# A transformer layer on one NeuronCore: the mixer's weight matrices laid out by the host in the blocks in which they are fetched

## The chip, the cores and the metric

The kernel runs on one core of one Trainium2 chip. The metric is the device time of one execution in microseconds (us), lower is better. All arrays come from HBM and the result goes back to HBM; what the host does to the inputs before the launch is not in the time.

## The reference

One layer on a sequence of 256 rows of 1024, in float32. A conditioning vector gives six modulation vectors. The mixer runs a gated linear recurrence and causal attention side by side on the modulated rows, and a mixture of 32 experts, two for each row, follows. Cut to what matters here:

```
mod = silu(c) @ w_ada + b_ada                  # w_ada 1024 x 6144: sh1, sc1, g1, sh2, sc2, g2
u    = normalize(x) * (1 + sc1) + sh1
proj = u @ w_in                                # w_in 1024 x 2560: x, y, q, k, v, 512 columns each
h    = rg_lru(conv(x)) * gelu(y)               # recurrence over time
att  = attention(q, k, v)
mix  = concat(rmsnorm(h), rmsnorm(att)) @ w_out   # w_out 1024 x 1024
x    = layernorm(alpha * x + g1 * mix)
x    = layernorm(alpha * x + g2 * experts(normalize(x) * (1 + sc2) + sh2))   # w1, w3, w2 of 32 experts
```

## The kernel before

**Slots.** An arena in SBUF holds five slots of 128 partitions x 4096 floats (16 KB of each partition, 2 MiB in all) and some work space; `slot(i)` is one of them. Each piece of a weight matrix that the mixer needs fills a slot and is used up before the next piece is fetched there. The experts' weights later use the same slots and three further buffers (`last`, `misc`, `fifth`).

**Fetches.** `load` (L224) fetches one slot in two DMAs of 1 MiB, one for each half of the partition's 16 KB. Which rows and columns go there is a rearranged view of the matrix in HBM (L220 to L222): the vectors sc1 (`V1[1, a]`, L254) come as 8 rows x 512 columns a partition, the vectors sh1, sc2 and g2 (`load_vec`) as 4 rows x 1024 columns, g1 and sh2 together (`load_ada`) as 2 rows x 2048 columns, the projections (`load_win`) as 8 rows x 512 columns, the output matrix (`load_wo`) as 4 rows x 1024 columns. So a partition's run of bytes that lie side by side in HBM is 2, 4, 8, 2 and 4 KB long in these five. The experts' w1, w3 and w2 lie in HBM so that a partition's 8 KB are one run.

**Order.** The program is written in the order in which each engine runs it; there is no planner. All of these fetches are issued by SyncE (SP) and go through one DMA queue, in order. SP waits before a fetch until the slot's last reader is done, and everything behind it waits too. The order at the start is x, `V1[1, 0]` (slot 0), half of W["x"] (slot 2), `V1[1, 1]` (slot 1), the other half of W["x"], `V1[0, 0]` and `V1[0, 1]` (slots 3 and 4), then W["y"] into slot 0 (L455), `pack_b`, W["q"] (L460), and so on: `AD[1, q]` (g1 and sh2), W["k"], W["v"], w_out, `V1[4]` and `V1[5]` (sc2 and g2).

**What uses them at the start.** TensorE transposes the normalized x, `scale_mm(0)` (L365) multiplies `V1[1, 0]`, `proj_T(0, ...)` (matmuls L430) projects x with W["x"]. Ahead of the matmuls each row block of a projection is split into two float32r parts, the high one by ScalarE (L407 or L410) and the rest by VectorE (L408 or L411). `vec_cols(0)` (L381, L387) turns `V1[0, 0]` and `V1[0, 1]` into the shift; VectorE adds it in L465, L467 copies it, L481 multiplies it with W["x"], and the projection of y begins. Between `vec_cols(0)` and L465 stands `ahead(9)` (L459): VectorE's L408 on the first row block of W["y"] comes ahead of L465 on its queue.

**Later.** Two modulation vectors go through HBM and back (`mod2_out` L660, `mod2_in` L664, both on SP; SP waits in L664 until the first has landed). The fetches of the first experts' weights (`load_static`, L859) need expert numbers that VectorE writes in L562 and SP reads (L856). The long run of expert units (L1212, L1355) fetches 8 KB rows in `bring_all` (L1166, L1169), the last group in halves.

Of the kernel before, what the change touches and what calls it, by code (L numbers as in the profile page):

```python
# [21 lines left out]
S, D = 256, 1024  # L22
H, DH = 8, 64
NE, DE = 32, 256
KD = D // 128
# [112 lines left out]
def arrays_of(inputs):  # L138
    i = {k: np.asarray(v) for k, v in inputs.items()}
    a, b, wg, rb, ln = pack_inputs(i)  # L140
    r = {k: np.ascontiguousarray(i[k]) for k in ("x", "w_ada", "w_in", "w_out", "w1", "w3", "w2")}
    r["b_ada"] = np.ascontiguousarray(i["b_ada"].reshape(12, 512))
    r["pack_a"], r["pack_b"], r["w_gate"], r["rb"], r["ln"] = a.array(), b.array(), wg, rb, ln
    return r, a.at, b.at
# [3 lines left out]
def layer(ctx: ExitStack, tc: tile.TileContext, at_a, at_b, x, w_ada, b_ada, w_in, w_out, w1, w3, w2,  # L148
          pack_a, pack_b, w_gate, rb, ln, out, dbg=None):
    nc = tc.nc  # L150
    te, ve, se, ge, sy = nc.tensor, nc.vector, nc.scalar, nc.gpsimd, nc.sync
# [34 lines left out]
    def slot(i):  # L186
        return arena[:, i * 4096:(i + 1) * 4096]
# [6 lines left out]
    def bank(pool=None):  # L194
        turn[0] += 1
        return (pool or (psx, psp)[turn[0] % 2]).tile([128, 512], F32, name="b")
# [11 lines left out]
    def A(name):  # L208
        o, w = at_a[name]
        return pka[:, o:o + w]  # L210
# [6 lines left out]
        o = at_a["par"][0] + PAR[name] + m  # L217
        return pka[:, o:o + n]

    ada = w_ada[0].rearrange("(p k) n -> p k n", k=KD)  # L220
    win = w_in[0].rearrange("(k p) n -> p k n", p=128)
    wov = w_out[0].rearrange("(k p) n -> p k n", p=128)  # L222

    def load(s, src):  # L224
        n, w = src.shape[1:]
        t = (slot(s) if isinstance(s, int) else s).rearrange("p (k n) -> p k n", k=n)
        for h in range(2):
            q = slice(h * n // 2, (h + 1) * n // 2)
            sy.dma_start(t[:, q], src[:, q])
        return t  # L230

    def load_vec(v, q, s):
        return load(s, ada[:, 4 * q:4 * q + 4, v * D:(v + 1) * D])

    def load_ada(g, q, s):
        return load(s, ada[:, 2 * q:2 * q + 2, g * 2048:(g + 1) * 2048])

    def load_win(j, s):
        return load(s, win[:, :, j * 512:(j + 1) * 512])

    def load_wo(j, s):
        return load(s, wov[:, 4 * j:4 * j + 4])

    se.dma_start(pka, pack_a)
    rbt = misc[:NB + 1, 3072:3464]
# [3 lines left out]
    AD, W = {}, {}  # L249
    V1 = {}  # L250

    W["x"] = slot(2).rearrange("p (k n) -> p k n", k=KD)
    for a in range(2):
        V1[1, a] = load(a, ada[:, :, D + a * 512:D + a * 512 + 512])  # L254
        sy.dma_start(W["x"][:, 4 * a:4 * a + 4], win[:, 4 * a:4 * a + 4, 0:512])
    V1[0, 0] = load_vec(0, 0, 3)
    V1[0, 1] = load_vec(0, 1, 4)
    ident = A("ident")

# [117 lines left out]
    def vec_cols(v):  # L377
        pa = abank()
        for k in range(KD):
            for j in range(4):  # L380
                te.matmul(pa[32 * j:32 * j + 32, 0:256], cd[:, k], V1[v, k // 4][:, k % 4, j * 256:(j + 1) * 256],  # L381
                          start=(k == 0), stop=(k == KD - 1), skip_group_check=True, tile_position=(0, 32 * j))
        r = tmp.tile([128, 256], F32, name="row", bufs=1)
        ve.tensor_copy(r, pa[:, 0:256])
        p = bank(psx)
        for s in range(2):
            te.matmul(p[:, s:8:2], r[:, s * 128:(s + 1) * 128], sel4, start=True, stop=True)  # L387
        return p[:, 0:8]
# [10 lines left out]
    def rows_of(w, scale=None):  # L399
        units.extend((w, k, scale) for k in range(KD))  # L400
# [18 lines left out]
    def proj_T(u, pool, after=None, mid=None, most=None, late=()):  # L419
        bs = [bank(pool) for _ in range(2)]  # L420
        for k in range(KD):
            ahead(most(k) if most else u + k + 4)
            t = split[u + k]
            products = [(m, a, b) for m in range(4) for a, b in parts3]
            if k in late:
                products.sort(key=lambda v: v[1])
            for n, (m, a, b) in enumerate(products):
                if mid and n == 6:
                    mid(k)
                te.matmul(half(bs, m), t[:, a, m * 128:(m + 1) * 128], ul[:, b, k], start=(k + m % 2 + a + b == 0),  # L430
                          stop=(k == KD - 1 and a == 1), skip_group_check=True)
            if after:
                after(k)
        return bs
# [18 lines left out]

    px = proj_T(0, psp, after_x, mid_x, lambda k: 4 if k < 4 else 8, (0, 4))
    W["y"] = load_win(1, 0)  # L455
    sy.dma_start(pkb, pack_b)
    rows_of(W["y"])
    p = vec_cols(0)
    ahead(9)  # L459
    W["q"] = load_win(2, 3)  # L460
    sy.dma_start(wgt, w_gate)
    ge.memset(brows[:, 0], 0.0)
    sy.dma_start(brows[0:128:32, 0], b_ada[4:8])
    AD[1, 0] = load_ada(1, 0, 1)
    ve.tensor_add(mod1[:, 0], p, A("bcol")[:, 0:8])  # L465
    shd = misc[:, 3072:3328].rearrange("p (k n) -> p k n", k=KD)
    ve.tensor_copy(shd, mod1[:, 0, :, None].to_broadcast([128, KD, 32]))  # L467
# [11 lines left out]
    for k in range(KD):  # L479
        j = k % 4  # L480
        te.matmul(pb[32 * j:32 * j + 32], shd[:, k], W["x"][:, k], start=(k < 4), stop=(k >= 4), skip_group_check=True,  # L481
                  tile_position=(0, 32 * j))
    W["k"] = load_win(3, 2)
    sy.dma_start(T, bass.AP(tensor=vrd.tensor, offset=vrd.offset, ap=[[1, 128], [384, H], [1, 256]]))
    AD[1, 1] = load_ada(1, 1, 4)
    rowx = brows[:, 1]
    xb = ch.tile([128, 4], F32, name="xb")
    xl, xc = t4(0), t4(1)
# [86 lines left out]
    def ada_mm(g, q, pt):  # L575
        for k in range(2):
            for j in range(4):
                te.matmul(pt[32 * j:32 * j + 32], cd[:, 2 * q + k], AD[g, q][:, k, j * 512:(j + 1) * 512],  # L578
                          start=(q == 0 and k == 0), stop=(q == 3 and k == 1), skip_group_check=True, tile_position=(0, 32 * j))
# [83 lines left out]
    def mod2_in(t, i):  # L663
# [3 lines left out]
    kT = nx[:, 1].rearrange("p (m t) -> p m t", m=4)  # L667
    pa1 = abank()
    ada_mm(1, 0, pa1)
    AD[1, 2] = load_ada(1, 2, 1)  # L670
    rows_of(W["k"])
    pq = proj_T(16, psp, after_q)
    AD[1, 3] = load_ada(1, 3, 3)
    qh = [qT[:, 2 * b:2 * b + 2].rearrange("p a b -> p (a b)") for b in range(2)]
    se.activation(qh[0], pq[0], AF.Copy, scale=DH ** -0.5)
    ve.tensor_scalar(qh[1], pq[1], DH ** -0.5, None, op0=OP.mult)
    ada_mm(1, 1, pa1)
    V1[4, 0] = load_vec(4, 0, 4)
    rows_of(W["v"])
    ge.memset(brows[:, 1], 0.0)  # L680
    sy.dma_start(brows[0:128:32, 1].rearrange("p (v n) -> p v n", v=2),
                 b_ada[8:12].rearrange("(v a) (h n) -> (a h) v n", v=2, h=2))
    pk = proj_T(24, psp, after_k)
    wo = [load_wo(0, 2)]
    ada_mm(1, 2, pa1)
    ada_mm(1, 3, pa1)
    wo.append(load_wo(1, 1))
    V1[4, 1] = load_vec(4, 1, 3)
    for b in range(2):
# [436 lines left out]
    p = bank(psp)  # L1126
# [66 lines left out]
    for k in range(KD):  # L1193
        q, sc, sh = pgs[k // 4][:, k % 4 * 128:k % 4 * 128 + 128], mod2p[:, 1, k:k + 1], mod2p[:, 0, k:k + 1]
# [551 lines left out]
```

## Time and profile before

| | |
|---|---|
| median of 3 runs | 307.99 us (307.07 to 308.94) |
| the profiled execution | 308.57 us, of which its span (first to last instruction) is 306.8 us |
| TensorE busy | 279.2 us (91%) |
| VectorE, ScalarE, GpSimd busy | 183.0, 108.9, 24.4 us |
| moved by DMA | 112.22 MB, mean 366 GB/s |
| granted TensorE clock | 0.99 on average |

How to read it: an engine's busy time tells how much of the span it worked, not whether the work sets the end. Two resources stand near full here, TensorE and the DMA engines, so the profile must be read stage by stage: which wait ends last there. L12 is line 12 of the kernel; `out<-in` names the tiles; SPq is SyncE's queue. A DMA's time to landing runs from its issue and contains all that stands ahead of it in the queue.

### The profile page before, as it was taken

The numbers are of one execution on the slowest core, as the hardware profiler recorded it, in microseconds if no ns is written. First come the engines' busy times: TensorE is split into PE (matmuls) and PEld (weight loads), VectorE is DVE, ScalarE is ACT, GpSimd is POOL, SyncE is SP. The second block draws the span as 40 slices with busy tenths as digits, with TensorE's granted clock in tenths as the row PEclk, the third lists the DMA queues.
The fourth block names the chain that finished last, engine by engine and source line by source line (L and its number), as shares of the span: only waits on it lengthen the run. The fifth ranks groups of instructions, "written<-read, shape, count | busy, mean of one in ns | idle before, by whom it ended". The sixth has DMA issues, their size and how long they took to land.

```text
span 306.8 us, 6105 instructions
## 1 busy us (share of the span) xinstructions
PE 279.2 (91%) x2344; PEld 186.3 (61%) x2344; DVE 183.0 (60%) x445; ACT 108.9 (35%) x230; POOL 24.4 (8%) x62
## 2 busy tenths in 40 slices
PE   0799999999999999999998999999999999959980
PEld 0578679897957644566475578585648455715430
DVE  2766188927786785888698790636273516250490
ACT  1233188778745452051438241123112211210110
POOL 0100632000010000000120200000000001200000
PEclk9999999999999999999999999999999999997998
DMA  7999999999999699899979999999999999999104
GB/s 271 388 392 407 395 396 401 385 394 426 406 409 407 237 419 418 316 424 347 311 246 424 366 414 425 420 420 424 420 419 421 418 420 420 422 412 395 49 4 146
DMA packets 26163, 112.22 MB, mean 366 GB/s; under 512 B 2253, under 2 KB 3586, under 8 KB 17420
## 3 DMA queue, kind: packets, MB, share of 16 engines
q1 hardware_dynamic: 25424, 110.74, 91.3%
q10 hardware_dynamic: 636, 0.99, 0.9%
q8 instruction: 20, 0.33, 0.4%
q14 instruction: 19, 0.16, 0.1%
q0 software_dynamic: 64, 0.01, 0.0%
HBM read 110.51 MB, written 1.22 MB: 364 GB/s over the span
## 4 chain that ended last, share of the span: by engine, by line
PE 57%; DMA 26%; DVE 11%; issue 1%; ACT 1%; POOL 0%; SPq 0%; DVEq 0%; ACTq 0%
DMA arena<-in_w 12%; PE b L430 11%; PE m L1212 10%; PE b L804 7%; DMA misc<-in_w 6%; DMA arena<-in_w_in 6%; PE m L1355 5%; PE b L779 4%; PE m L1286 3%; PE a L578 2%; PE a L1212 2%; PE acc L1309 2%; PE a L590 2%; DMA pka<-in_pack_a 1%; PE a L365 1%
## 5 line engine op out<-in xcount | busy, mean ns | idle before, releaser
L430 PEld LDWEIGHTS b<-ul,w 128*128 128x128 f32 x384 | 46.6, 192 | 4.2 <-ACT w L407 1.7
L430 PE MATMUL b<-ul,w 128*128 128x256 f32 x384 | 48.4, 285 | 0.5 <-ACT w L410 0.5
L1212 PE MATMUL m<-arena,xg 128*64 128x256 f32 (+1 forms) x288 | 38.4, 401 | 3.8 <-DMA arena<-in_w 3.8
L1212 PEld LDWEIGHTS m<-arena,xg 128*64 128x64 f32 (+1 forms) x288 | 21.9, 131 | 14.1 <-DMA arena<-in_w 4.7
L408 DVE TENSOR_TENSOR w<-arena,w 128x512 fp32r<-128x512 f32 x32 | 21.9, 698 | 13.9 <-ACT w L407 13.7
L1355 PE MATMUL m<-arena,hT 128*32 128x512 f32 (+2 forms) x184 | 29.1, 596 | 0.5 <-ACT hT L1333 0.5
L804 PE MATMUL b<-arena,mT 128*128 128x512 f32 x64 | 29.0, 601 | 0.0
L407 ACT ACTIVATE w<-arena 128x512 fp32r<-128x512 f32 x32 | 19.5, 625 | 12.4 <-DMA arena<-in_w_in 6.3
L1327 DVE TENSOR_TENSOR hh<-hh,m 128x256 f32<-128x256 f32 x7 | 2.9, 421 | 34.7 <-ACT hh L1326 34.7
L1212 PE MATMUL m<-fifth,xg 128*32 128x256 f32 (+1 forms) x96 | 23.2, 401 | 0.0
L1212 PE MATMUL m<-misc,xg 128*32 128x256 f32 (+1 forms) x160 | 21.3, 380 | 0.0
L1368 ACT ACTIVATE yh<-ys 128x256 fp32r<-128x256 f32 (+1 forms) x22 | 10.5, 493 | 29.8 <-DVE ys L1367 26.0
L804 PEld LDWEIGHTS b<-arena,mT 128*128 128x128 f32 x64 | 11.6, 190 | 13.0 <-issue 12.8
L1367 DVE SCALAR_TENSOR_TENSOR ys<-m,ws,g2b 128x256 f32<-128x256 f32 (+1 forms) x22 | 12.0, 578 | 12.1 <-PE m L1355 11.9
L1326 ACT ACTIVATE hh<-m 128x256 f32<-128x256 f32 x7 | 2.7, 384 | 46.3 <-PE m L1212 46.3
L1355 PEld LDWEIGHTS m<-arena,hT 128*32 128x32 f32 (+2 forms) x184 | 8.5, 120 | 16.7 <-issue 13.5
L1286 PE MATMUL m<-oh,xa 128*128 128x256 f32 (+1 forms) x64 | 15.6, 284 | 0.0
L1286 PE MATMUL m<-oh,xb 128*128 128x256 f32 (+1 forms) x64 | 15.4, 280 | 0.0
L1212 PE MATMUL m<-last,xg 128*32 128x256 f32 x64 | 14.2, 380 | 0.0
L1212 PEld LDWEIGHTS m<-fifth,xg 128*32 128x32 f32 (+1 forms) x96 | 11.7, 125 | 3.5 <-issue 1.4
L1212 PEld LDWEIGHTS m<-misc,xg 128*32 128x32 f32 (+1 forms) x160 | 13.3, 126 | 0.8
L728 ACT ACTIVATE s<-s,z 128x128 f32<-128x128 f32 (+1 forms) x16 | 7.1, 449 | 18.3 <-DVE z L726 18.3
(322 smaller groups left out, 495.4 us busy)
## 6 DMA issues: line engine op xcount, KB each, us to landing
arena<-in_w SPq DMA_DIRECT2D x41, 1024.0 KB, 14.8
arena<-in_w_ada SPq DMA_DIRECT2D x22, 1024.0 KB, 13.9
arena<-in_w_in SPq DMA_DIRECT2D x10, 1024.0 KB, 15.2
last<-in_w SPq DMA_DIRECT2D x6, 1024.0 KB, 15.2
misc<-in_w SPq DMA_DIRECT2D x6, 1024.0 KB, 14.2
fifth<-in_w SPq DMA_DIRECT2D x6, 1024.0 KB, 15.8
arena<-in_w_out SPq DMA_DIRECT2D x4, 1024.0 KB, 10.4
arena<-in_w SPq DMA_DIRECT2D x8, 512.0 KB, 12.7
```

The source lines that it names most:

```text
L407: se.activation(t[:, 0], w[:, k], AF.Copy)
L408: ve.tensor_sub(t[:, 1], w[:, k], t[:, 0])
L430: te.matmul(half(bs, m), t[:, a, m * 128:(m + 1) * 128], ul[:, b, k], start=(k + m % 2 + a + b == 0), stop=(k == KD - 1 and a == 1), skip_ ...
L578: te.matmul(pt[32 * j:32 * j + 32], cd[:, 2 * q + k], AD[g, q][:, k, j * 512:(j + 1) * 512], start=(q == 0 and k == 0), stop=(q == 3 and k ...
L728: se.activation(s3[:, c], s3[:, c], AF.Exp, bias=z[:, c:c + 1], accum_out=z[:, 4 + c:5 + c])
L779: te.matmul(pvv[i], ul[:, ua, k, i * 128:(i + 1) * 128], t[:, wa], start=(k + wa + ua == 0), stop=(k == KD - 1 and wa == 1))
L804: te.matmul(p, mT[:, k, i * 128:(i + 1) * 128], wo[k // 4][:, k % 4, h * 512:(h + 1) * 512], start=(m == 0), stop=(m == 3))
L1212: te.matmul(ph[o:o + w, a * 256:(a + 1) * 256], xs[:, k, o:o + w], place[q][0].rearrange("p (a k f) -> p a k f", a=2, k=KD)[:, a, k], star ...
L1286: te.matmul(q, nhl[i][:, a, k * 128:(k + 1) * 128], oh[:, i, :n], start=(a + i == 0), stop=(a + i == 2))
L1355: te.matmul(ps[h][o:o + w], hT[:, j, o:o + w], place[q][1][:, j * 1024 + h * 512:j * 1024 + (h + 1) * 512], start=(j == 0), stop=(j == 1), ...
L1367: ve.scalar_tensor_tensor(ys[:, o:o + q], p[:, o:o + q], ws, g2b[:, sl], op0=OP.mult, op1=OP.mult)
L1368: se.activation(yh[:, sl], ys[:, o:o + q], AF.Copy)
```

## The change

The host reshapes and stacks `w_ada`, `w_in` and `w_out` into blocks of 128 x 4096 floats, one for each slot's content, in which a partition's 16 KB lie side by side. `load` takes a block and fetches it as two halves of 2048 columns: 128 runs of 8 KB, one every 16 KB. The count, size, order and destination of the DMAs and all the work on the engines stay; the views of the slots in SBUF are the same as before. The loads of g1 and sh2 (`load_ada`) had 8 KB runs already, 192 KB from one partition to the next.

```diff
-    r = {k: np.ascontiguousarray(i[k]) for k in ("x", "w_ada", "w_in", "w_out", "w1", "w3", "w2")}
+    r = {k: np.ascontiguousarray(i[k]) for k in ("x", "w1", "w3", "w2")}
+
+    ada, win = i["w_ada"][0].reshape(128, KD, -1), i["w_in"][0].reshape(KD, 128, -1).transpose(1, 0, 2)
+    wo = i["w_out"][0].reshape(KD, 128, -1).transpose(1, 0, 2)
+    blocks = [ada[:, :, h * 512:h * 512 + 512] for h in (2, 3)]
+    blocks += [ada[:, 2 * q:2 * q + 2, 2048:4096] for q in range(4)]
+    blocks += [ada[:, 4 * q:4 * q + 4, v * D:v * D + D] for v in (0, 4, 5) for q in range(2)]
+    r["w_ada"] = np.stack([b.reshape(128, 4096) for b in blocks])
+    r["w_in"] = np.stack([win[:, :, j * 512:j * 512 + 512].reshape(128, 4096) for j in range(5)])
+    r["w_out"] = np.stack([wo[:, 4 * j:4 * j + 4].reshape(128, 4096) for j in range(2)])
...
-    def load(s, src):
-        n, w = src.shape[1:]
-        t = (slot(s) if isinstance(s, int) else s).rearrange("p (k n) -> p k n", k=n)
+    def load(s, src, n):
+        t = slot(s) if isinstance(s, int) else s
         for h in range(2):
-            q = slice(h * n // 2, (h + 1) * n // 2)
+            q = slice(h * 2048, (h + 1) * 2048)
             sy.dma_start(t[:, q], src[:, q])
-        return t
+        return t.rearrange("p (k n) -> p k n", k=n)
+
+    def load_scale(a, s):
+        return load(s, w_ada[a], 8)
 
     def load_vec(v, q, s):
-        return load(s, ada[:, 4 * q:4 * q + 4, v * D:(v + 1) * D])
-
-    def load_ada(g, q, s):
-        return load(s, ada[:, 2 * q:2 * q + 2, g * 2048:(g + 1) * 2048])
+        return load(s, w_ada[max(6, 2 * v) + q], 4)
+
+    def load_ada(q, s):
+        return load(s, w_ada[2 + q], 2)
 
     def load_win(j, s):
-        return load(s, win[:, :, j * 512:(j + 1) * 512])
+        return load(s, w_in[j], 8)
 
     def load_wo(j, s):
-        return load(s, wov[:, 4 * j:4 * j + 4])
+        return load(s, w_out[j], 4)
...
-        V1[1, a] = load(a, ada[:, :, D + a * 512:D + a * 512 + 512])
-        sy.dma_start(W["x"][:, 4 * a:4 * a + 4], win[:, 4 * a:4 * a + 4, 0:512])
+        V1[1, a] = load_scale(a, a)
+        sy.dma_start(slot(2)[:, a * 2048:(a + 1) * 2048], w_in[0][:, a * 2048:(a + 1) * 2048])
```

## Rows read from the trace of the kernel before

**Rows 1.** The page: what the DMA engines moved in each fortieth of the span (slices 0 to 39, 7.67 us each), and the queue that carries SP's and ScalarE's DMAs.

```profile
GB/s 271 388 392 407 395 396 401 385 394 426 406 409 407 237 419 418 316 424 347 311 246 424 366 414 425 420 420 424 420 419 421 418 420 420 422 412 395 49 4 146
...
q1 hardware_dynamic: 25424, 110.74, 91.3%
```

**Rows 2.** The DMA view's issues: destination and source, count, size of each, median us from issue to landing. These are all the fetches that the change touches.

```profile
arena<-in_w_ada SPq DMA_DIRECT2D x22, 1024.0 KB, 13.9
arena<-in_w_in SPq DMA_DIRECT2D x10, 1024.0 KB, 15.2
...
arena<-in_w_out SPq DMA_DIRECT2D x4, 1024.0 KB, 10.4
...
last<-in_w_ada SPq DMA_DIRECT2D x2, 1024.0 KB, 11.5
```

**Rows 3.** Stretches of the span: start and end in us, length, busy time of each engine with the count of instructions, granted TensorE clock, mean busy share of the DMA engines, GB/s. In the first stretch the queue carries 2 KB runs, in the second mostly 4 KB runs, in the third the experts' 8 KB runs; the fourth carries 8 KB runs too, while the queue runs empty in between.

```profile
12.00:20.00 8.00, 7.32 (x82) 5.59 (x83) 3.68 (x8) 3.56 (x7) 0.00 (x0) 1.00 1.05 387
85.00:97.00 12.00, 12.00 (x85) 7.23 (x78) 8.02 (x12) 7.57 (x18) 1.48 (x2) 1.00 1.03 408
172.00:276.00 104.00, 100.00 (x860) 62.09 (x848) 50.20 (x128) 23.73 (x53) 3.18 (x4) 1.00 1.01 419
138.00:150.00 12.00, 12.00 (x54) 6.64 (x52) 8.84 (x27) 4.50 (x8) 1.33 (x3) 1.00 0.97 330
```

**Rows 4.** The chain of work that ended last, around the first wait for a weight: start us, us, what.

```profile
13.90 3.62 PE a L365 x64
...
18.16 19.14 DMA arena<-in_w_in
...
39.22 1.93 PE b L481 x16
```

**Rows 5.** The timeline of all engines from 33.5 to 39.5 us, the instructions around the same place: start us, us, engine, line, operation, tiles, count, and in brackets how long the engine was idle before it and who ended that.

```profile
33.78 3.66 PE L381 MATMUL a<-arena,cd 128*32 128x256 f32 x64
...
37.41 0.63 ACT L407 ACTIVATE w<-arena 128x512 fp32r<-128x512 f32 x1 [6.34 <-DMA arena<-in_w_in]
37.51 0.42 DVE L384 COPY row<-a 128x256 f32<-128x256 f32 x1 [5.86 <-PE a L381]
...
37.99 0.61 PE L387 MATMUL b<-pka,row 128*128 128x4 f32 x4 [0.55 <-DVE row L384]
38.07 0.69 DVE L408 TENSOR_TENSOR w<-arena,w 128x512 fp32r<-128x512 f32 x1
...
38.68 0.16 DVE L465 TENSOR_TENSOR mod<-b,pka 128x8 f32<-128x8 f32 x1
```

**Rows 6.** The DMA view's issues of two narrow stretches. First 16.7 to 16.8 us: the second half of `V1[0, 1]`, issued at 16.75 us, beside the first half, of which no landing is known. Then 18.1 to 18.3 us: the first half of W["y"], issued at 18.16 us.

```profile
arena<-in_w_ada SPq DMA_DIRECT2D x2, 1024.0 KB, 17.7
...
arena<-in_w_in SPq DMA_DIRECT2D x1, 1024.0 KB, 19.1
```

**Rows 7.** TensorE's timeline, three runs of the projections' matmuls.

```profile
27.83 6.02 PE L430 MATMUL b<-ul,w 128*128 128x256 f32 x48 [0.24 <-ACT w L410]
...
46.30 7.43 PE L430 MATMUL b<-ul,w 128*128 128x256 f32 x60
...
72.85 11.77 PE L430 MATMUL b<-ul,w 128*128 128x256 f32 x96
```

**Rows 8.** The waits of all compute engines from 39 to 170 us, all of the list that name a DMA: who waited for what, us in total, times, longest.

```profile
PEld b L481 <- DMA pkb<-in_pack_b: 0.3, 1, 0.3
...
PEld b L804 <- DMA arena<-in_w_ada: 0.2, 1, 0.2
PEld a L590 <- DMA mod2p<-mod2d: 0.2, 1, 0.2
PEld a L590 <- DMA arena<-in_w_ada: 0.2, 1, 0.2
```

**Rows 9.** SP's timeline from 84 to 128 us: when it issued which DMAs.

```profile
88.98 0.54 SPq L660 DMA_DIRECT2D mod2d<-misc  x1
101.68 0.34 SPq L664 DMA_DIRECT2D mod2p<-mod2d  x1
102.11 0.90 SPq L229 DMA_DIRECT2D arena<-in_w_ada  x2
...
111.89 0.93 SPq L859 DMA_DIRECT2D arena<-in_w  x2
...
126.96 1.20 SPq L859 DMA_DIRECT2D arena<-in_w  x2
```

**Rows 10.** SP's waits from 84 to 170 us: line, what ended the wait, us in total, times, longest.

```profile
SPq L664 <- DMA mod2d<-misc: 20.1, 2, 12.1
...
SPq L859 <- PE a L590: 5.5, 5, 3.0
...
SPq L856 <- DVE eos L562: 3.1, 1, 3.1
```

**Rows 11.** Stretches again, columns as in rows 3: two places where the DMA engines stand still in part.

```profile
97.00:104.00 7.00, 7.00 (x60) 5.26 (x58) 5.07 (x15) 3.62 (x12) 0.74 (x1) 1.00 0.66 232
...
125.00:130.00 5.00, 5.00 (x75) 2.67 (x77) 3.88 (x8) 0.00 (x0) 0.54 (x1) 1.00 0.72 255
```

**Rows 12.** The chain again: the first expert unit's matmuls, and the first of the three DMA pieces behind which the chain stands until 276 us.

```profile
165.99 7.24 PE a L1212 x128
...
219.86 16.77 DMA arena<-in_w
```

More of the change, by code (lines that the diff above doesn't have):

```diff
@@ L218, in P @@
         return pka[:, o:o + n]
-    ada = w_ada[0].rearrange("(p k) n -> p k n", k=KD)
-    win = w_in[0].rearrange("(k p) n -> p k n", p=128)
-    wov = w_out[0].rearrange("(k p) n -> p k n", p=128)
-    def load(s, src):
-        n, w = src.shape[1:]
-        t = (slot(s) if isinstance(s, int) else s).rearrange("p (k n) -> p k n", k=n)
+    def load(s, src, n):
+        t = slot(s) if isinstance(s, int) else s
         for h in range(2):
-            q = slice(h * n // 2, (h + 1) * n // 2)
+            q = slice(h * 2048, (h + 1) * 2048)
             sy.dma_start(t[:, q], src[:, q])
-        return t
+        return t.rearrange("p (k n) -> p k n", k=n)
+    def load_scale(a, s):
+        return load(s, w_ada[a], 8)
     def load_vec(v, q, s):
-        return load(s, ada[:, 4 * q:4 * q + 4, v * D:(v + 1) * D])
-    def load_ada(g, q, s):
-        return load(s, ada[:, 2 * q:2 * q + 2, g * 2048:(g + 1) * 2048])
+        return load(s, w_ada[max(6, 2 * v) + q], 4)
+    def load_ada(q, s):
+        return load(s, w_ada[2 + q], 2)
     def load_win(j, s):
-        return load(s, win[:, :, j * 512:(j + 1) * 512])
+        return load(s, w_in[j], 8)
     def load_wo(j, s):
-        return load(s, wov[:, 4 * j:4 * j + 4])
+        return load(s, w_out[j], 4)
     se.dma_start(pka, pack_a)
@@ L463, in layer @@
     sy.dma_start(brows[0:128:32, 0], b_ada[4:8])
-    AD[1, 0] = load_ada(1, 0, 1)
+    AD[1, 0] = load_ada(0, 1)
     ve.tensor_add(mod1[:, 0], p, A("bcol")[:, 0:8])
@@ L484, in layer @@
     sy.dma_start(T, bass.AP(tensor=vrd.tensor, offset=vrd.offset, ap=[[1, 128], [384, H], [1, 256]]))
-    AD[1, 1] = load_ada(1, 1, 4)
+    AD[1, 1] = load_ada(1, 4)
     rowx = brows[:, 1]
@@ L669, in layer @@
     ada_mm(1, 0, pa1)
-    AD[1, 2] = load_ada(1, 2, 1)
+    AD[1, 2] = load_ada(2, 1)
     rows_of(W["k"])
     pq = proj_T(16, psp, after_q)
-    AD[1, 3] = load_ada(1, 3, 3)
+    AD[1, 3] = load_ada(3, 3)
     qh = [qT[:, 2 * b:2 * b + 2].rearrange("p a b -> p (a b)") for b in range(2)]
```

## The prediction

> **What bounds the kernel now.** I read the page's line of GB/s first [rows 1]: the DMA engines move about 390 to 420 GB/s in nearly every slice, and the main queue's packets fill 91% of the span. That looks like a kernel bound by its transfers. But the line has holes, slice 13, counted from 0 (237, from 100 us), and slices 16, 18, 19 and 20 (316, 347, 311, 246, to 161 us). A queue that runs empty there has forgotten how early it was before. So I ask for each stage which wait ends last. The chain of waits has one DMA link ahead of the holes: the first half of W["y"], issued at 18.16 us and landed 19.14 us later, at 37.30 us [rows 4]. The next DMA link begins at 219.86 us [rows 12], behind the holes and among the experts' weights, which the change does not touch. Between the two, the list of waits from 39 to 170 us names a DMA four times, 0.2 to 0.3 us each [rows 8]. From 39 to 102 us TensorE sets the pace: its projection matmuls take 0.124, 0.123 and 0.125 us each in runs of 60, 96 and 48 [rows 7], the same whether the fetches are near or far. From there to 166 us the chain goes through VectorE and TensorE alone; then the first expert unit begins [rows 12].
>
> **The fetches themselves.** The change touches 38 DMAs of 1 MiB [rows 2]. A MiB (1.0486 MB) of 2 KB runs takes 1.0486/0.387 = 2.71 us, of 4 KB runs 1.0486/0.408 = 2.57 us, of 8 KB runs 1.0486/0.419 = 2.50 us, by the stretches in which each kind fills the queue [rows 3]. 4 MiB of w_ada (sc1) and all 10 of w_in go from 2 KB to 8 KB runs: 14 x 0.21 = 2.9 us. 12 MiB of w_ada (sh1, sc2, g2) and 4 of w_out go from 4 to 8 KB: 16 x 0.07 = 1.1 us. The 8 MiB of g1 and sh2 had 8 KB runs: nothing. In all the queue is busy **4.0 us** less, all of it ahead of 120 us.
>
> The unknown is the new spacing: 8 KB runs 16 KB apart stand nowhere in the trace. The nearest rows are the experts' 8 KB runs at 2.50 us a MiB. The far end is the slowest stretch of 8 KB runs, 330 GB/s, 3.18 us [rows 3]. I take 2.50, since that slow stretch has a queue that keeps running dry, and the early queue does not. Below 2.50 I see no source of a gain: that is the rate of the fullest stretch of the trace.
>
> The Trainium skill gives a mechanism for long runs: "DMA: Bandwidth & Descriptors", "Why small descriptors are slow", charges each packet some 3 cycles beside one for every 32 bytes. By that my estimate is 67 against 64.75 cycles for 2 KB, 3.4%, and 1.1% for 4 KB runs: 1.3 + 0.5 = 1.8 us of queue time instead of 4.0. The trace differs from it in size: 387 to 419 GB/s is 8% [rows 3]; I go by the trace.
>
> **Start, to 39 us.** The x rows and the first constants stand ahead of all changed fetches in the queue, so the start to 13.9 us stays. scale_mm(0) and the first projection never wait for a fetch in the chain [rows 4]. W["y"]'s first half has 6 MiB of 2 KB runs, 4 MiB of 4 KB runs and itself ahead: 7 x 0.21 + 4 x 0.07 = 1.7 us earlier, landing at 35.6 us. What this is worth is seen in the timeline [rows 5]. ScalarE splits the first row block at 37.41, VectorE follows with L408 at 38.07, and L465, the shift, comes behind that at 38.68. But L465 also needs TensorE: vec_cols(0) runs from 33.78 to 37.44 us (64 matmuls at 0.057 us), VectorE copies the row at 37.51, L387 runs from 37.99 to 38.60. With W["y"] 1.7 us earlier L408 moves into VectorE's idle 5.86 us ahead of L384 [rows 5], and L465 then starts at 38.60 at the earliest: a gain of **0.08 us at most**, and I take 0.05. So the wait for W["y"] goes, and vec_cols is late next by the same amount. Nor does vec_cols wait for its own data: the second half of V1[0, 1] lands at 16.75 + 17.7 = 34.45 us [rows 6] and is used in the last quarter of the 64 matmuls, from 33.78 + 48 x 0.057 = 36.5 us.
>
> **From 39 to 102 us.** All fetches land up to 4 us earlier and nobody waits for them [rows 7, 8]: **0**. The cover is TensorE's own work; were it gone, the four waits of rows 8 are the most to be had, 0.9 us together, and they lie under a busy TensorE.
>
> **SP.** The same 38 DMA instructions in the same order. Its queue is what gives the time back. mod2_out waits behind some 12 us of fetches (issued 88.98, and L664 issues at 101.68 [rows 9]); this wait, of 20.1 us in two [rows 10], gets shorter by up to 3 us, so V1[5, 0], which stands behind it on SP, leaves at about 98 to 99 us instead of 102.11. Then the gain meets gates that no fetch moves: the first static experts leave at 111.89, once VectorE has written their numbers (L562) and SP has read them, and the third expert leaves at 126.96, when TensorE's L590 has let go of its slot [rows 9, 10]. The DMA engines already stand still in part from 125 to 130 us, at a share of 0.72 [rows 11]; with everything ahead 4 us earlier, this hole grows from 1.4 us to about 5. **0**.
>
> **The end.** From 172 to 276 us the queue carries the experts' rows at 419 GB/s [rows 3], without a hole, and sets the end. Its start is set by compute: the first of these fetches goes once the matmuls of the first unit, from 165.99 us [rows 12], free a buffer. Moved by the same 0.05 us as the chain ahead of it.
>
> **Sum.** 308.57 - 0.05 = 308.5 us for the profiled execution, of which 306.8 is span. Its own time is 0.58 us above the median of the runs shown, so the median goes from 307.99 to **307.9 us**. I call a difference under 0.5% (1.5 us) no change: the three runs shown spread by 0.6%, and a measurement of this kernel can tell about that.
>
> **Rivals.** (1) **The bandwidth counts whole.** If the kernel is bound by the sum of its transfers, 4.0 us less of queue time comes off the end: 308.0 - 4.0 = 304.0 us. For it: 91% busy, and the end is a transfer [rows 1, 12]. Against it: the holes, in which the queue waits for TensorE and VectorE. Chance 0.10.
> (2) **The first wait counts whole.** If W["y"] alone holds L465, and vec_cols only seems tied because the ends of matmuls are modelled, the 1.7 us pass through TensorE's unbroken stretch to the end: 306.3 us. For it: the chain names this DMA [rows 4]. Against it: L384 waited for TensorE until 37.5 whatever W["y"] did [rows 5]. Chance 0.07.
> (3) **The new spacing is slow**, and the time is worse. Its place is the same landing, where the slack is nil today. The 11 MiB up to it now take 7 x 2.71 + 4 x 2.57 = 29.3 us. The rival decides from 1.6 us more, that is 2.81 us a MiB or 373 GB/s; at 3.18 us it costs 35.0 - 29.3 = 5.7 us: 308.0 + 5.7 = 313.7 us. For it: no row shows runs 16 KB apart. Against it: g1 and sh2, 8 KB runs 192 KB apart, leave no mark on the line of GB/s (385 to 426 in slices 1 to 12) [rows 1]. Chance 0.08.
> The Trainium skill has a rule on this side, in "DMA: Bandwidth & Descriptors", "Latency and other measured facts": a row pitch of a large power of two in HBM costs rate, 207 GB/s at 512 KiB and less beyond it. 16 KiB is not in its list, and no run here shows it yet; at 207 GB/s my estimate is 5.07 us a MiB, 26 us at W["y"] and a time of 334 us.
> That the blocks are not fetched in longer runs than before can be left out: the code says 2048 floats of a row that lie side by side.
>
> **How the numbers follow.** Forecast 0.75, rivals 0.10, 0.07, 0.08. Faster is (1) and (2), 0.17; slower is (3), 0.08. The range takes in the forecast with the spread of runs (307 to 309) and reaches to (2) below, 305.9 to 309.4 us; it leaves out (1) and (3), 0.18.
>
> **What would show it.** Right: the early slices of GB/s rise from 385 to 407 to about 410 to 420; packets under 8 KB fall; W["y"] lands near 35.6 us, and ScalarE's L407 starts then, while L465 stays at 38.6; L664 and V1[5, 0] go out 3 to 4 us earlier; the static experts' issues at 111.9 and 127.0 stay, and the share from 125 to 130 us falls below 0.72; the first expert unit starts at 166 us. Wrong: L465 moved by over 0.3 us; a start of the first expert unit earlier by over 1 us; early slices that do not rise, or fall under 373 GB/s.

## The result, and the profile after

The changed kernel takes 306.41 us (median of 20 executions, 303.38 to 307.05), the kernel before 307.72 us (20 executions, 305.44 to 310.34). The ratio is 0.9949, 95% interval 0.9927 to 0.9971: 0.9 to 2.2 us less, at the border of what was called no change. (Medians are of all executions; ratios and counts of executions leave out those more than 1.5% above the fastest of their kernel, in the three later measurements 14 of before's 93 and none of after's, so that the ratios rather understate the gain.) The profiled execution of after took 306.76 us, its span is 304.9 us against 306.8 before. Lines of the code stand 7 higher in after: L465 is L472, L1212 is L1219.

The page of after: GB/s in fortieths of the span, and the main queue; beside [rows 1].

```profile
GB/s 284 426 426 415 419 416 417 396 421 423 415 393 308 340 379 418 196 425 336 339 232 419 366 419 427 422 417 423 419 420 419 419 422 420 417 415 399 102 3 148
...
q1 hardware_dynamic: 18000, 110.74, 89.8%
```

The same bytes go in 18,000 packets, not 25,424, and slices 1 to 6 rise from 388–407 to 415–426. The holes stay and move forward: slice 12 is now low too, slice 16 fell from 316 to 196.

Stretches of after, columns as in [rows 3]; the last two are the holes of [rows 11].

```profile
12.00:20.00 8.00, 7.24 (x86) 5.76 (x87) 4.27 (x9) 4.14 (x8) 0.00 (x0) 1.00 1.00 417
...
172.00:276.00 104.00, 100.25 (x860) 62.25 (x852) 49.94 (x127) 23.73 (x53) 3.18 (x4) 1.00 1.01 419
...
97.00:104.00 7.00, 7.00 (x59) 5.09 (x59) 5.01 (x18) 3.34 (x11) 0.86 (x1) 1.00 0.60 217
125.00:130.00 5.00, 5.00 (x85) 2.99 (x88) 4.50 (x10) 0.00 (x0) 0.54 (x1) 1.00 0.52 167
```

The early queue carries 417 GB/s where it carried 387, the experts' stretch is the same 419, and a part of the time saved shows in the holes: 0.60 and 0.52 of the DMA engines busy, where it was 0.66 and 0.72.

The first half of W["y"] in after, issued at 16.61 us (the DMA view's issues, 16.6 to 16.7 us; last number: us to landing). It lands at 35.2 us, 2.1 us earlier than before [rows 4, 6].

```profile
arena<-in_w_in SPq DMA_DIRECT2D x1, 1024.0 KB, 18.6
```

The timeline's row of `scale_mm(0)` in before (3.62 us in the chain of [rows 4]):

```profile
13.83 3.64 PE L365 MATMUL a<-arena,cd 128*32 128x128 f32 x64
```

The timeline of after from 33 us, beside [rows 5]; its first row below is `scale_mm(0)`.

```profile
13.97 2.91 PE L372 MATMUL a<-arena,cd 128*32 128x128 f32 x64
...
33.20 3.66 PE L388 MATMUL a<-arena,cd 128*32 128x256 f32 x64
...
35.30 0.63 ACT L414 ACTIVATE w<-arena 128x512 fp32r<-128x512 f32 x1 [4.81 <-DMA arena<-in_w_in]
...
36.93 0.42 DVE L391 COPY row<-a 128x256 f32<-128x256 f32 x1 [5.85 <-PE a L388]
37.27 0.68 DVE L415 TENSOR_TENSOR w<-arena,w 128x512 fp32r<-128x512 f32 x1
37.41 0.61 PE L394 MATMUL b<-pka,row 128*128 128x4 f32 x4 [0.55 <-DVE row L391]
38.05 0.17 DVE L472 TENSOR_TENSOR mod<-b,pka 128x8 f32<-128x8 f32 x1
```

ScalarE has its row block 2.1 us earlier, and the shift (L472) comes 0.63 us earlier, at 38.05: as soon as TensorE's L394 ends, at 38.02. TensorE's branch itself is earlier, because the 64 matmuls of `scale_mm(0)` took 2.91 us instead of 3.64. No fetch holds the shift here any more.

The chain of after, beside [rows 4, 12], has no fetch of W["y"]:

```profile
14.04 2.90 PE a L372 x64
...
37.41 0.62 PE b L394 x4
...
38.60 1.92 PE b L488 x16
...
165.36 7.24 PE a L1219 x128
...
219.23 15.93 DMA arena<-in_w
```

The first expert unit starts 0.63 us earlier too, so between the shift and it nothing was gained or lost. SP's timeline of after, beside [rows 9]:

```profile
88.36 0.54 SPq L667 DMA_DIRECT2D mod2d<-misc  x1
98.53 0.33 SPq L671 DMA_DIRECT2D mod2p<-mod2d  x1
98.95 0.86 SPq L233 DMA_DIRECT2D arena<-in_w_ada  x2
...
111.25 0.92 SPq L866 DMA_DIRECT2D arena<-in_w  x2
...
126.32 1.20 SPq L866 DMA_DIRECT2D arena<-in_w  x2
```

The fetches behind `mod2_in` go out 3.2 us earlier; the two gates behind them move by 0.64 us, which is the head's gain and no more.

### The profile page after: what moved, and what is told of

Read it like the earlier page. It is cut to its first block, busy times and chain, and to the rows that moved or that the text cites. A ratio compares the mean times of both kernels' runs of the same rounds, so it can differ in the third digit from the quotient of the medians.

```text
span 304.9 us, 6099 instructions
## 1 busy us (share of the span) xinstructions
PE 278.5 (91%) x2344; PEld 185.9 (61%) x2344; DVE 183.0 (60%) x445; ACT 108.9 (36%) x230; POOL 24.5 (8%) x62
## 4 chain that ended last, share of the span: by engine, by line
PE 63%; DMA 20%; DVE 11%; ACT 2%; issue 1%; POOL 0%; SPq 0%; ACTq 0%; DVEq 0%
PE b L437 15%; DMA arena<-in_w 12%; PE m L1219 10%; PE b L811 7%; DMA misc<-in_w 6%; PE m L1362 5%; PE b L786 4%; PE m L1293 3%; PE a L585 2%; PE a L1219 2%; PE acc L1316 2%; PE a L597 2%; PE a L372 2%; DMA pka<-in_pack_a 2%; PE a L388 1%
## 5 line engine op out<-in xcount | busy, mean ns | idle before, releaser
L1219 PE MATMUL m<-arena,xg 128*64 128x256 f32 (+1 forms) x288 | 38.4, 401 | 3.1 <-DMA arena<-in_w 3.1
L415 DVE TENSOR_TENSOR w<-arena,w 128x512 fp32r<-128x512 f32 x32 | 21.9, 700 | 13.7 <-ACT w L414 13.7
L1219 PEld LDWEIGHTS m<-arena,xg 128*64 128x64 f32 (+1 forms) x288 | 21.9, 131 | 13.5 <-DMA arena<-in_w 4.1
L1219 PE MATMUL m<-fifth,xg 128*32 128x256 f32 (+1 forms) x96 | 23.2, 401 | 0.0
L1219 PE MATMUL m<-misc,xg 128*32 128x256 f32 (+1 forms) x160 | 21.3, 380 | 0.0
L1362 PEld LDWEIGHTS m<-arena,hT 128*32 128x32 f32 (+2 forms) x184 | 8.5, 120 | 16.7 <-issue 13.5
L1219 PE MATMUL m<-last,xg 128*32 128x256 f32 x64 | 14.2, 380 | 0.0
L1219 PEld LDWEIGHTS m<-fifth,xg 128*32 128x32 f32 (+1 forms) x96 | 11.7, 125 | 3.5 <-issue 1.4
L1219 PEld LDWEIGHTS m<-misc,xg 128*32 128x32 f32 (+1 forms) x160 | 13.3, 126 | 0.8
L735 ACT ACTIVATE s<-s,z 128x128 f32<-128x128 f32 (+1 forms) x16 | 7.1, 448 | 18.3 <-DVE z L733 18.3
```

The lines of the kernel that those rows point to most:

```text
L415: ve.tensor_sub(t[:, 1], w[:, k], t[:, 0])
L735: se.activation(s3[:, c], s3[:, c], AF.Exp, bias=z[:, c:c + 1], accum_out=z[:, 4 + c:5 + c])
L1219: te.matmul(ph[o:o + w, a * 256:(a + 1) * 256], xs[:, k, o:o + w], place[q][0].rearrange("p (a k f) -> p a k f", a=2, k=KD)[:, a, k], star ...
L1362: te.matmul(ps[h][o:o + w], hT[:, j, o:o + w], place[q][1][:, j * 1024 + h * 512:j * 1024 + (h + 1) * 512], start=(j == 0), stop=(j == 1), ...
```

## The experiments

**Theory A.** Of the two branches that end in the shift, W["y"]'s splits and TensorE's `vec_cols(0)`, the second is not fixed: TensorE gets to its full rate earlier in one execution than in another. The profiled execution of before is one in which it got there late, so that the branches tied; in others the shift waits for W["y"], and the change takes that wait away. **Theory B.** The gain comes from a later part of the queue, which is busy 4 us less. **Theory C**, as the expectations use it, is chance: no gain. Rival (2) of the prediction, by which W["y"] sets the shift in every execution, stands beside these. The kernels are named by their labels; the ratio is always to the kernel before, on the same chip.

**Which blocks matter.** Each of two kernels has both forms of the matrices in HBM and fetches only some pieces as blocks.

```diff
# e1_head_blocks: blocks for sc1, W["x"], sh1 and W["y"], rows for all else; e2_rest_blocks: the reverse
+    return load_block(s, b_w_in[j], 8) if HEAD == (j == 1) else load_rows(s, win[:, :, j * 512:(j + 1) * 512])
```

> Blocks only for what is fetched up to W["y"] (sc1, W["x"], sh1, W["y"]); W["q"], W["k"], W["v"], g1 and sh2, sc2, g2 and w_out are fetched as in the kernel before. Theory A (tie at W["y"]): TensorE's matmuls reach full rate earlier in some executions than in the profiled one of before; there vec_cols ends earlier and the landing of W["y"] at 37.3 us is what the shift waits for. Then this kernel has the whole gain of the change: ratio about 0.995, W["y"] at 35.2. Theory B (the gain comes from the queue being early later on, in the hand-over to the experts' fetches around 170 us): no gain, ratio 0.999 to 1.001. Theory C (the gain is chance): 1.000 here and everywhere.

> The complement of the kernel with blocks at the head: sc1, W["x"], sh1 and W["y"] are fetched as before, all the others in blocks. Theory A: no gain, ratio 0.999 to 1.001. Theory B: the whole gain, about 0.995, or most of it (1.4 of 4.0 us of queue time lie here for certain, up to 2.2). Theory C: 1.000.

Measured: e1 306.24 us (before 307.23), ratio 0.9958, 0.9923 to 0.9994; e2 307.61 us, ratio 1.0018, 0.9987 to 1.0049. The blocks ahead of W["y"] and its own keep the gain; the other 26 MiB, with half of the 4 us of queue time (2.1 us by the prediction's rates: 6 MiB from 2 KB runs, 12 from 4 KB runs), give none. Theory B falls: e2's interval leaves out the 0.995 that it asked for. Against theory C stand the intervals of after and e1, which leave out 1. The timeline of e2's profiled execution shows the wait that the profile of before hides:

```profile
13.71 1.95 PE L387 MATMUL a<-arena,cd 128*32 128x128 f32 x64
...
36.16 0.61 PE L409 MATMUL b<-pka,row 128*128 128x4 f32 x4 [0.55 <-DVE row L406]
...
37.11 0.63 ACT L429 ACTIVATE w<-arena 128x512 fp32r<-128x512 f32 x1 [7.86 <-DMA arena<-in_w_in]
37.77 0.69 DVE L430 TENSOR_TENSOR w<-arena,w 128x512 fp32r<-128x512 f32 x1 [1.67 <-ACT w L429]
38.38 0.16 DVE L487 TENSOR_TENSOR mod<-b,pka 128x8 f32<-128x8 f32 x1
...
38.92 1.92 PE L503 MATMUL b<-arena,misc 128*32 128x512 f32 x16 [2.16 <-DVE misc L489]
```

Here `scale_mm(0)` took 1.95 us, so TensorE's branch was done at 36.77; VectorE then stood 1.67 us for ScalarE's split, and that for the fetch. The shift came at 38.38, 1.6 us after TensorE was ready. The profiled execution of e1 is of the other kind (3.64 us, shift at 38.91 though W["y"] was split at 35.71), which speaks against rival (2): there W["y"] sets nothing.

**Making TensorE early on purpose.** 22 matmuls on constants, written to a bank that is not in use yet, ahead of the first stage.

```diff
     pv = bank(psp)
+    for _ in range(22):
+        te.matmul(pv[:, 0:128], onesf, onesf, start=True, stop=True)
```

> The kernel before, with 22 matmuls on a constant tile on TensorE ahead of its transposes, from about 1.5 us, so that its matmuls run at full rate in every execution when the transposes begin. They change no result. TensorE's branch to the shift gets shorter by some 1.7 us for scale_mm(0) (64 matmuls in 1.95 instead of 3.64 us) and up to 2 us for the transposes. Theory A: W["y"] at 37.3 us now holds the shift in all executions; L465 at 38.6 as in the profiled run, a gain of at most 0.1 us against the profiled run, ratio about 0.997 to 1.000. Were the fetch of no account: L465 2 to 3 us earlier and a ratio of 0.990 to 0.993.

> The changed kernel with the same 22 matmuls. Theory A: W["y"] lands at 35.2 us, so the shift can come down to about 36.5 us against 38.1 in the changed kernel's profile; ratio to the kernel before about 0.989 to 0.991, and 1.5 to 2 us ahead of the kernel before with the same matmuls. Theory B or C: the two kernels with these matmuls differ by as much as without them, 0.5% or nothing.

Measured: e3 (put into before) 308.61 us, ratio 1.0031, 0.9997 to 1.0066; e4 (put into after) 306.10 us, ratio 0.9954, 0.9918 to 0.9989. Rows of e3's timeline:

```profile
13.24 1.95 PE L367 MATMUL a<-arena,cd 128*32 128x128 f32 x64
...
34.85 0.59 PEld L383 LDWEIGHTS a<-arena,cd 128*32 128x32 f32 x16 [0.61 <-DMA arena<-in_w_ada]
...
36.47 0.61 PE L389 MATMUL b<-pka,row 128*128 128x4 f32 x4 [0.55 <-DVE row L386]
37.62 0.63 ACT L409 ACTIVATE w<-arena 128x512 fp32r<-128x512 f32 x1 [8.40 <-DMA arena<-in_w_in]
...
38.90 0.16 DVE L467 TENSOR_TENSOR mod<-b,pka 128x8 f32<-128x8 f32 x1
...
39.44 2.58 PE L483 MATMUL b<-arena,misc 128*32 128x512 f32 x16 [2.36 <-DVE misc L469]
```

and of e4's:

```profile
35.92 0.61 PE L396 MATMUL b<-pka,row 128*128 128x4 f32 x4 [0.55 <-DVE row L393]
...
36.74 0.16 DVE L474 TENSOR_TENSOR mod<-b,pka 128x8 f32<-128x8 f32 x1
...
37.28 1.92 PE L490 MATMUL b<-arena,misc 128*32 128x512 f32 x16 [0.75 <-DVE misc L476]
```

The same early TensorE brings the shift to 36.74 with the blocks, and leaves it at 38.90 without them. That is theory A at work. TensorE's own branch stands for a fetch too in e3, 0.61 us in the last quarter of `vec_cols(0)`, for `V1[0, 1]`; in e4 it does not. And e3 shows a second cost. After the wait of 2.36 us the matmuls L483 took 2.58 us instead of 1.92; e3's stretches show why (the number ahead of the DMA share is the granted clock):

```profile
37.10:39.40 2.30, 0.00 (x0) 0.00 (x0) 1.06 (x3) 0.94 (x2) 0.60 (x2) 1.00 1.04 399
40.60:44.00 3.40, 3.40 (x17) 2.06 (x10) 2.90 (x6) 2.12 (x5) 0.43 (x1) 0.50 1.05 387
44.00:60.00 16.00, 16.00 (x135) 14.43 (x134) 12.51 (x27) 13.51 (x25) 2.60 (x5) 1.00 1.05 396
```

TensorE did nothing for 2.3 us; from 40.6 us, 1.2 us after its matmuls had begun again, its clock was granted at 0.50 (1.2 of 2.4 GHz) for 3.4 us. Neither time came out as expected. e3 was expected at 0.997 to 1.000, and the second cost, which the expectation left out, is of the right sign. For e4 the expectation was a ratio of 0.989 to 0.991. Its profiled execution has a span of 302.3 us, but most of its others a lower mean clock; what the added matmuls set off there was not profiled.

**The old layout, the first piece alone.** W["y"] is fetched in three DMAs, so that its first row block lands ahead of the rest.

```diff
-    W["y"] = load_win(1, 0)
+    W["y"] = slot(0).rearrange("p (k n) -> p k n", k=KD)
+    for k0, k1 in ((0, 1), (1, 4), (4, 8)):
+        sy.dma_start(W["y"][:, k0:k1], win[:, k0:k1, 512:1024])
```

> The kernel before, every byte fetched in the old runs, but the first row block of W["y"] (256 KB) goes in a DMA of its own ahead of the other seven: it lands about 2 us earlier, at 35.3 us, as in the changed kernel, while the queue is no less busy. Theory A (tie at W["y"]): the gain of the change comes back without the change, ratio 0.994 to 0.997. Any theory by which the shorter queue time itself counts: 0.999 to 1.002.

Measured: 306.62 us (before 307.88), ratio 0.9963, 0.9923 to 1.0004. Without a byte laid out anew, ScalarE's split starts at 35.24 us, much as in after (35.30):

```profile
35.24 0.63 ACT L407 ACTIVATE w<-arena 128x512 fp32r<-128x512 f32 x1 [3.92 <-DMA arena<-in_w_in]
```

The central value is close to those of e1 and after; the interval just reaches 1.

**The other way.** W["y"] goes behind `pack_b` and `w_gate`, in before and in after.

```diff
-    W["y"] = load_win(1, 0)
     sy.dma_start(pkb, pack_b)
+    sy.dma_start(wgt, w_gate)
+    W["y"] = load_win(1, 0)
...
     W["q"] = load_win(2, 3)
-    sy.dma_start(wgt, w_gate)
```

> The kernel before with pack_b and w_gate (1096 KB in all) fetched ahead of W["y"] instead of behind it and behind W["q"]: W["y"] lands 2.7 to 2.9 us later, at about 40.1 us; all bytes and instructions stay. Theory A: the shift waits for it in every execution, 2.5 to 2.8 us later, and no slack takes it up to the end: ratio 1.008 to 1.009. If the early wait were hidden: 1.000 to 1.003.

> The changed kernel with the same two fetches ahead of W["y"]: it lands at about 38.0 us, 0.7 us later than in the kernel before. Theory A: the change loses its whole gain and a little more, ratio 1.000 to 1.003 to the kernel before, though every fetch is in blocks. If the queue time itself counts: 0.995 to 0.997, as without the two.

Measured: e6 310.60 us, ratio 1.0105, 1.0061 to 1.0150; e7 309.54 us, ratio 1.0049, 1.0016 to 1.0083; both lie above what was expected (1.008 to 1.009, 1.000 to 1.003). In e7 W["y"] landed at 37.93 us, 0.6 us later than in before, and it is slower than before by a like amount as after is faster: all the blocks are in place, and no gain is left. e6's timeline and two of its stretches:

```profile
39.90 0.63 ACT L407 ACTIVATE w<-arena 128x512 fp32r<-128x512 f32 x1 [8.76 <-DMA arena<-in_w_in]
...
41.17 0.16 DVE L465 TENSOR_TENSOR mod<-b,pka 128x8 f32<-128x8 f32 x1
...
41.71 3.58 PE L481 MATMUL b<-arena,misc 128*32 128x512 f32 x16 [3.04 <-DVE misc L467]
```

```profile
38.70:41.70 3.00, 0.00 (x0) 0.00 (x0) 1.06 (x3) 0.97 (x2) 0.85 (x3) 1.00 1.06 388
41.70:45.10 3.40, 3.39 (x16) 0.59 (x16) 2.60 (x6) 2.81 (x6) 0.74 (x1) 0.50 1.05 387
```

Again a wait, of 3.0 us, then half the clock. The shift is 2.5 us later than in before, the first expert unit (170.13 us) 4.1 us. The profiled execution of e7, the longest of its twelve, shows the same in the new layout: a wait of 2.27 us, and half the clock from 39.0 to 45.8 us.

```profile
39.84 3.64 PE L488 MATMUL b<-arena,misc 128*32 128x512 f32 x16 [2.27 <-DVE misc L474]
```

```profile
39.00:45.80 6.80, 5.96 (x27) 2.98 (x28) 4.58 (x11) 3.74 (x7) 0.74 (x1) 0.50 1.01 418
```

**The shift ahead of VectorE's split**, the layout of before:

```diff
     p = vec_cols(0)
-    ahead(9)
...
     ve.tensor_copy(shd, mod1[:, 0, :, None].to_broadcast([128, KD, 32]))
+    ahead(9)
```

> The kernel before with the split of W["y"]'s first row block written behind the shift and its copy, so that L465 and L467 don't stand behind L408 on VectorE; no fetch changes. Theory A: where W["y"] is late, the shift and L481 go up to 1.5 us earlier, but the projection's first matmul still needs the row block at about 38.7 us, and ScalarE's part of the first modulated block stands behind the split: part of the gain, 0.996 to 0.999. If the landing were not what holds the shift: 1.000.

Measured: 306.76 us, ratio 0.9975, 0.9942 to 1.0007. In its profiled execution L464, the shift, follows L387 at once (37.86 us), though ScalarE's first split of W["y"] (L407) began at 37.17 only:

```profile
37.21 0.61 PE L387 MATMUL b<-pka,row 128*128 128x4 f32 x4 [0.55 <-DVE row L384]
37.86 0.17 DVE L464 TENSOR_TENSOR mod<-b,pka 128x8 f32<-128x8 f32 x1 [0.70 <-PE b L387]
```

By the central value it gives half of the gain; by its interval this stays unclear.

**After once more, and the clock at the end.** The profile of after has a stretch at half the clock from 275.4 us, as before has near the same place. e9 is after unchanged; e10 puts 11 matmuls on the identity between the groups of the last unit; e11 adds to e10 the 22 matmuls, the first row block of W["y"] alone and the shift first.

```diff
                 for o, w, q in groups:
+                    for _ in range({64: 3, 96: 8}.get(o, 0) if fill and a + k == 0 else 0):
+                        te.matmul(ph[:, 256:384], ident, ident, start=True, stop=True, ...)
```

> The changed kernel once more, beside the next two. Theory A: ratio 0.994 to 0.997 as at first; chance: 1.000.

> The changed kernel with 3 and 8 matmuls on a constant tile inside the last expert unit, where TensorE waits 0.8 and 1.9 us for the experts' weights; they change no result. If it is a wait of TensorE after which its clock falls to half for some us (as behind the waits for W["y"] and, in the profiled executions of before and after, behind the wait at 275 us), the fall at 275 us becomes rarer and the executions that had it get 1.5 to 2 us faster: ratio 0.989 to 0.993 to the kernel before. If the fall has nothing to do with the wait: as the changed kernel, 0.994 to 0.997, or slower where the added matmuls delay the waiting ones.

> The changed kernel with all that helped or could help: the fills in the last unit, 22 matmuls at the start for TensorE's rate, W["y"]'s first row block in a DMA of its own, and the shift ahead of the split. Theory A: W["y"] lands at 33.3 us and never holds the shift, which TensorE's branch allows at 36.4 us instead of 37 to 38.6: 0.7 to 1.5 us beyond the kernel with the fills in the last unit, ratio 0.985 to 0.990.

Measured against 307.51 us of before: e9 306.19, ratio 0.9976 (0.9943 to 1.0008); e10 305.10, 0.9923 (0.9887 to 0.9958); e11 304.65, 0.9920 (0.9888 to 0.9952), where 0.985 to 0.990 was expected. A second measurement of after thus gives 1.3 us by the medians, as the first does, but 0.7 by the ratio (the first: 1.6), just short of what was expected and with an interval that reaches 1. e10 and e11 are faster than before clear of the noise. Why e11 missed is not known: seven of its twelve executions have a mean clock of 0.988 or less, and the profiled one is not among them. Stretches at the end, first of e9, then of e10:

```profile
274.00:280.00 6.00, 4.51 (x52) 2.42 (x56) 0.26 (x2) 0.00 (x0) 0.00 (x0) 0.72 1.02 404
```

```profile
274.00:280.00 6.00, 6.00 (x90) 4.17 (x92) 0.64 (x2) 0.00 (x0) 0.00 (x0) 1.00 1.02 407
```

With TensorE kept busy in its waits the clock is whole there: in this execution the 6 us hold 90 matmul records, 16 of them of added matmuls, instead of 52. One profile would not decide it, since e1 and e2 have a whole clock there with nothing added; but all 12 executions of e10 have a mean clock of 0.992 or more, and nine of e9's 12 have 0.991 or less.

**The profiled executions side by side** (us; without that of e7, whose clock fell in both places: shift 39.30, first unit 169.39; the shift from the timeline, the first expert unit from the chain; falls: stretches of granted clock 0.50 at 40 to 46 us, "head", or at 275 to 280 us, "tail"):

| kernel | `scale_mm(0)` | shift | first unit | unit less shift | span end less unit | falls |
|---|---|---|---|---|---|---|
| before | 3.64 | 38.68 | 165.99 | 127.3 | 140.8 | tail |
| after | 2.91 | 38.05 | 165.36 | 127.3 | 139.5 | tail |
| e9 | 3.15 | 38.39 | 165.76 | 127.4 | 139.5 | tail |
| e1 | 3.64 | 38.91 | 166.20 | 127.3 | 137.6 | none |
| e2 | 1.95 | 38.38 | 165.69 | 127.3 | 137.7 | none |
| e5 | 3.64 | 38.87 | 166.45 | 127.6 | 140.8 | tail |
| e8 | 2.62 | 37.86 | 165.20 | 127.3 | 140.3 | tail |
| e4 | 1.96 | 36.74 | 164.07 | 127.3 | 138.2 | none |
| e10 | 3.64 | 38.85 | 166.16 | 127.3 | 137.9 | none |
| e11 | 1.95 | 36.66 | 164.21 | 127.6 | 138.0 | none |
| e3 | 1.95 | 38.90 | 167.74 | 128.8 | 138.1 | head |
| e6 | 3.64 | 41.17 | 170.13 | 129.0 | 136.9 | head |

From the shift to the first expert unit it is 127.3 to 127.6 us whatever the layout, and 1.5 to 1.7 us more where the clock fell behind the wait. So a microsecond of the shift is a microsecond of the unit, and a wait behind which the clock fell cost its length and about 1.6 us. A fall in the tail goes with a later end, 140.2 against 137.8 us behind the unit on average, in the new layout and in the old.

## Why the prediction was right, and where it failed

The median came out at 306.41 us, within the range of 305.9 to 309.4, but 1.5 us under the forecast of 307.9; the gain is 1.6 us by the ratio and 1.3 by the medians, 0.7 and 1.3 in the second measurement, where the sum had 0.05. That the range holds is in part luck: its lower bound was drawn below rival (2), whose 306.3 the median nearly met, while the forecast's own reason for no gain did not hold. Point by point:

**Queue time.** 4.0 us less: right in kind and, up to W["y"], a little small. The early stretch rose from 387 to 417 GB/s, and the 11 MiB up to W["y"], 29.3 us by the prediction, took 2.1 us less; by this estimate that is 27.2 us or 2.47 us a MiB (424 GB/s), where 2.50 was taken. The rule of the Trainium skill ("DMA: Bandwidth & Descriptors", "Why small descriptors are slow") made 3.4% of 2 KB runs; 387 to 417 is 8%, so the rows were the better guide.

**Start: the step that failed.** "A gain of 0.08 us at most" took the tie of one profiled execution for the state of all. It holds for executions like that one (e1, e5: `scale_mm(0)` 3.64 us, the shift at 38.9 whatever W["y"] does). But the same 64 matmuls, with the same work ahead of them, took 2.91, 3.15, 2.62 and 1.95 us in others (after, e9, e8, e2); vec_cols follows by as much, and with the old layout the shift then waits at 38.4 to 38.9 (e2, e3) while TensorE is ready up to 1.8 us before. With the blocks it can follow TensorE (36.74 in e4). So the mechanism was neither the forecast's (nothing) nor rival (2) (1.7 us always), but rival (2)'s wait in a part of the executions. Nor does it always hold that vec_cols does not wait for its own data: in e3 it stood 0.61 us. What the wait is in other executions could not be read from [rows 5]. That the two branches ended within 0.1 us of each other could, and should have raised rival (2)'s chance: whatever TensorE's branch gains over such a tie in another execution is lost to the wait.

**A detail of the same step** was wrong without a price: VectorE's split was to move ahead of L384. It can't, `vec_cols(0)` stands ahead of `ahead(9)` in the program. In after L415 runs right behind L391, at 37.27, beside TensorE's L394.

**39 to 102 us: 0.** Right. In after one wait from 38 to 170 us names a DMA, 0.3 us:

```profile
PEld b L488 <- DMA pkb<-in_pack_b: 0.3, 1, 0.3
```

From 102 to 166 us the chain of before does not go through VectorE and TensorE alone, as the prediction has it; ScalarE's L728 and L766 have 1.6 us of it. Nothing hangs on that.

**SP and the holes: 0.** Right, with its numbers: `mod2_in` leaves 3.2 us earlier, the gates at 111.25 and 126.32 only 0.64, and the share from 125 to 130 us falls from 0.72 to 0.52. Most of the 4.0 us of queue time went into the holes. The stretch that holds them, first of before, then of after:

```profile
95.00:165.00 70.00, 67.81 (x449) 40.99 (x448) 55.22 (x155) 26.92 (x72) 4.97 (x9) 1.00 0.91 349
```

```profile
95.00:165.00 70.00, 67.78 (x448) 41.49 (x444) 55.81 (x159) 26.89 (x69) 5.09 (x9) 1.00 0.87 333
```

16 GB/s less over 70 us are 1.1 MB, by an estimate 2.7 us at 419 GB/s.

**The end** moved with the head, as said, by 0.63 us at the first unit: 0.7 less of `scale_mm(0)`, 0.14 more ahead of it by the chains. The prediction's own sign of error, a shift moved by over 0.3 us, was met. Of the 1.9 us between the two spans the other 1.3 lie behind the first unit, in code that is the same; single executions, both with a fall in the tail, and not explained.

**Rivals.** (1), the bandwidth counted whole, is refuted by the holes and by e2. (2), as it stood, is refuted by e1 and e10: W["y"] lands early there, and the shift still comes at 38.9 us, with TensorE. (3), slow 16 KB spacing, is refuted by 417 GB/s. The Trainium skill's rule on row pitches ("DMA: Bandwidth & Descriptors", "Latency and other measured facts"), measured there on copies from HBM to HBM, would have made this 334 us if it reached down to 16 KiB. It does not show at that spacing: the trace has 417 GB/s.

**What stays open** is how the gain splits. Over the nine rows of the table without matmuls added in the head, `scale_mm(0)` is on average 0.44 us under 3.64, which is about what the wait alone would cost before. Sorted by the mean granted clock of the execution, before had (three measurements) 28 of 79 at 0.994 or more, mean 305.97 us; 35 at 0.988 to 0.994, 307.48; 16 below, 308.70. After (two measurements, e9's included) had 11 of 32 at 304.89; 13 at 306.51; 8 at 306.68. So the gain is about 1.0 us with few falls of the clock and 2.0 with most. e3, in which the wait is forced, has 9 of its 11 in the lowest group (308.41), e10 none of 12. This fits a fall of the clock behind the wait for W["y"] in some of before's executions and none in after's, but no such execution of before was profiled: argued, not shown.

## What to carry to other kernels

A profile is one execution: where two branches tie in it, and one of them hangs on a matmul rate that rises at varying times, the other can be a wait in the executions that were not profiled, and may be worth shortening. Bandwidth saved is worth what the next waits on it are worth: here 4 us of queue time bought 0.7 to 1.6 us at one early landing, and one smaller first DMA in the old layout (e5) showed a gain of like size. Before such a layout change is made for its transfers, ask what stands at the next hole of the queue; here the holes took most of the rest.

## What the runs showed of the hardware

8 KB runs 16 KB apart are as quick as the experts' whole rows: 417 against 419 GB/s. TensorE's rise to its full rate differs from execution to execution: 64 equal matmuls took from 1.95 to 3.64 us behind the same work. The granted clock does not show this: it reads 1.00 from 12 to 20 us in before [rows 3] and in after alike. And a wait of TensorE can be paid twice: with 2.3 us (e3, e7) and 3.0 us (e6) without a matmul the clock went down to 0.50, in e7 before the wait was over, in e3 and e6 for 3.4 us, and about 1.6 us more were lost in these two; with 2.16 us in e2 it stayed whole:

```profile
38.90:42.30 3.40, 3.38 (x28) 1.94 (x29) 2.59 (x6) 3.31 (x7) 0.74 (x1) 1.00 1.03 429
```

The Trainium skill tells of waits for a DMA between bursts of matmuls, after which the next burst starts slow ("TensorE: Matmul & The Clock Gate", "HAM oscillation — how this bites in real kernels"); e3, e6 and e7 agree, e2 shows that not every wait of about this length does it. Eleven matmuls that compute nothing of use, put into the waits of the last unit, were worth about 1.1 us by the medians (306.19 to 305.10), though the two intervals overlap.
